# Landing figures of the load planner in a two-layer diffusion trunk: own values for stores, weights, reloaded operands and broadcast rows

## The chip, the cores and the metric

The kernel runs on one core of one Trainium2 chip. The metric is the device time of one execution in microseconds (us). Five engines work side by side on a core, each with its own queue of instructions: TensorE (PE: matmuls and transposes; its weight loads are listed as PEld), VectorE (DVE), ScalarE (ACT), GpSimd (POOL) and SyncE (SP). Here SP issues nearly all transfers (DMA). Data lie in HBM, in SBUF (128 partitions) and, for results of matmuls, in the eight banks of PSUM.

## The reference

One step of a diffusion model with two layers, for 128 context tokens and 512 latent tokens, model width 2048, all in float32. Per layer:

```python
shift, scale, gate = modulation(c, ada_w[l], ada_b[l])   # silu(c) @ w + b
h = rms_norm(x, norm_g[l]) * (1.0 + scale) + shift
y = mixer(h)                     # h @ w_in, branches, times silu(gate path)
x = x + gate * (y @ w_out[l])
```

Layer 0 mixes by windowed attention beside gated linear attention (GLA), layer 1 by neighbourhood attention beside a spatial-gating MLP (gMLP). A final norm follows. Context tokens have a conditioning vector of their own (`c_ctx`), so every modulation vector exists twice. Keys, values and the GLA states of the context are outputs too.

## The kernel before, in words

Activations are kept transposed: 16 tiles (k) of 128 features by 640 tokens. Every float32 operand of the large products is split into a high part in a rounded format and the remainder: `acth` and `actl` for activations, `whi` and `wlo` for weights. A product is then three matmuls (high by high, high by low, low by high) over two halves of 320 tokens. Later stages replace part of the plain products by Strassen-like ones, with sums of tiles in `eh`, `el`, `fh`, `fl`.

A weight tile of 128x512 goes through four steps: a load into `wraw`, `rs` or `adas` (SP), `whi` by ACT, `wlo` by POOL or DVE, matmuls by PE. Its slot in `wraw` can be loaded again when `wlo` is done.

Beside the matmuls runs a background task, `ada_task` (L1434), which works out the modulation vectors by dot products on DVE (and, while POOL helps, products on POOL that ACT sums up). It loads tiles of `ada_w` and, at the start of each column piece, two rows: the two conditioning vectors, each broadcast to all 128 partitions (`crow_s`; `shift_s` for the job "b0"). ACT copies each row to a PSUM bank. Three or four slots rotate, so the load that refills a slot is issued after the instruction that read it. The task runs the jobs "b0", "g0" (gate of layer 0) and "1" (shift and scale of layer 1) during layer 0, with pieces of 512 columns in `adas`; the job "g1" (gate of layer 1), with pieces of 256 columns in `rawx` and `small`, starts during layer 1 (`last_gate`, L2709). In the start, `shifts()` (L1622) does the same with `crow_b` and tiles `ada_s0`, while PE multiplies the tiles of `ada0` directly (L1599).

Between projections, `handover` (L1107) rewrites the operand of the next product: tiles which had been stored to HBM (`x1T_dram`, `yT_dram`) are loaded again, scaled where needed, split into `acth` and `actl`, and folded for the Strassen steps. PE needs them tile by tile. High and low parts of half an operand are also set aside in HBM and fetched back (`bh_dram`, `bl_dram`).

**What sets the order.** The order of instructions on every engine is made while the program is built, by a planner that keeps an estimated time of each engine (`Pace`, L56). Every operation that is emitted moves the estimated time of its engine on, and the estimated moment at which its output is ready is noted for each stretch of memory. `now` is the estimated time of PE. Generators for the side tasks are advanced in `tick` (L537) between matmuls. They ask the planner whether an operand is ready: `until` (L508) holds a task back until a tile is due within 0.05 us, and `wpump` (L748) emits a weight split only if its data are due within a lag. Nothing of this waits at run time: there, each engine takes its instructions in the order emitted, and semaphores hold an instruction until its operands are there.

Loads and stores go through `dma` (L473). A transfer whose operands are not ready by the estimate is put off; otherwise it is emitted, and its landing is estimated from the time `q` of the SP queue, the time `d` at which the DMA engines are free, the bytes, and a constant. The helpers `mm` and `tr` (L449 and L454 in the profile) emit matmuls and transposes; ACT, DVE and POOL instructions carry the line L219, and transfers L486.

Of the kernel before, what the change touches and what calls it, by code (L numbers as in the profile page):

```python
# [26 lines left out]
SPILL, YSP, KEEP, SHIFTS = "x1T_dram", "yT_dram", ("bh_dram", "bl_dram"), "shift_s"  # L27
# [218 lines left out]
class Trunk:  # L246
# [226 lines left out]
    def dma(self, out, in_):  # L473

        pc = self.pace
        o, i = [pc.span(out)], [pc.span(in_)]
        if pc.late:
            pc.due(o + i)
        n = int(np.prod(out.shape)) * 4
        rows = in_.name == SHIFTS  # L480

        def emit():
            at = pc.t["q"] = max(pc.t["q"], self.now, pc.ready("q", o, i)) + 0.45
            pc.t["d"] = max(pc.t["d"], at + 0.65) + max(0.09, n / 400e3)
            pc.note("q", o, i, pc.t["d"] + (self.ROWS if rows else 1.0))
            self.nc.sync.dma_start(out, in_)  # L486

        if pc.ready("q", o, i) <= self.now + 0.1:
            emit()
        else:  # L490
            pc.late.append((emit, o + i, lambda: pc.ready("q", o, i)))
# [2631 lines left out]
```

## Time and profile before

| What | Value |
|---|---|
| Median of 3 runs | 2054.4 us (2052.85 to 2056.66) |
| The profiled execution's own time | 2053.88 us |
| Its span, first to last instruction | 2052.1 us |
| Mean granted clock of TensorE | 0.997 |
| Instructions | 40329 |
| Moved by DMA | 344.13 MB, mean 168 GB/s |

The span is some 1.8 us shorter than the execution's time. The profile gives the busy time of each engine, the waits (who ended the idle time of whom), the chain of waits that ended last, the landing times of transfers, and any stretch of the timeline. "acth<-Y" means: writes acth, reads Y. A number in square brackets behind a row of the timeline is the idle time of that engine just before it, with what ended it. Stretches give for each engine the busy time and, in brackets, the count of instructions.

### The profile page before, as it was taken

The page shows a single profiled execution, that of the slowest core. Times are in us where ns is not written, and L with a number is a line of the kernel's source. Part 1 is how long each engine was busy: PE and PEld are TensorE (multiplying, and loading weights), DVE is VectorE, ACT ScalarE, POOL GpSimd, SP SyncE. Part 2 cuts the span into 40 slices and gives each one's busy share as a digit, 9 for nine tenths or more (in the row PEclk, how much of TensorE's full clock was granted, in tenths as well). Part 3 has the DMA queues.
Part 4 walks back from the last instruction along what each step waited for, and adds up shares of the span by engine and source line. Part 5 has one row for each costly group of instructions (what it writes and reads, how often), then busy time and mean ns, then how long its engine had stood idle before and what let it go on. Part 6 is the DMA issues. An engine that isn't in the chain of part 4 may idle for free.

```text
span 2052.1 us, 40329 instructions
## 1 busy us (share of the span) xinstructions
PE 2012.5 (98%) x14255; PEld 1975.3 (96%) x14255; DVE 1364.1 (66%) x3191; ACT 1093.2 (53%) x2414; POOL 1356.6 (66%) x1088
## 2 busy tenths in 40 slices
PE   8999999999999999999999999999999999999997
PEld 6899999999999999999989999999999999999997
DVE  4656578566667766897376787666666676568445
ACT  5445456444664765544465444555555654455443
POOL 4555345446456555888755777767766689878884
PEclk9999999999999999999999999999999999999999
DMA  9955333436567555575524434444344354266437
GB/s 381 394 206 167 120 105 107 129 114 203 154 210 225 171 169 179 192 230 188 188 92 149 127 117 134 143 132 134 110 154 132 116 165 151 92 216 195 146 95 277
DMA packets 234315, 344.13 MB, mean 168 GB/s; under 512 B 22048, under 2 KB 139648, under 8 KB 234112
## 3 DMA queue, kind: packets, MB, share of 16 engines
q1 hardware_dynamic: 232912, 340.38, 50.9%
q8 instruction: 112, 1.84, 0.4%
q10 hardware_dynamic: 1200, 1.17, 0.2%
q14 instruction: 91, 0.75, 0.1%
HBM read 304.99 MB, written 33.85 MB: 165 GB/s over the span
## 4 chain that ended last, share of the span: by engine, by line
PE 82%; DMA 9%; DVE 4%; ACT 2%; issue 1%; POOL 1%; SPq 0%; DVEq 0%; POOLq 0%; ACTq 0%
PE bank L449 80%; PE bank L454 2%; DMA more<-ada 1%; DMA Y<-xT 1%; DMA Y<-ada 1%; DMA wraw<-w_out 1%; DVE bank L219 1%; POOL wlo L219 1%; DMA wraw<-w_even 1%; DMA adas<-ada 1%; DMA raw<-ada_s 1%; DMA adas<-ada_g 1%; DVE adas L219 1%; DVE arena L219 1%; ACT whi L219 1%
## 5 line engine op out<-in xcount | busy, mean ns | idle before, releaser
L449 PE MATMUL bank<-acth,whi 128*128 128x320 f32 (+3 forms) x3072 | 939.8, 318 | 5.5 <-DVE YB L219 1.9
L449 PE MATMUL bank<-actl,whi 128*128 128x320 f32 (+3 forms) x3072 | 916.1, 310 | 2.0 <-POOL actl L219 2.0
L449 PE MATMUL bank<-acth,wlo 128*128 128x320 f32 (+3 forms) x3072 | 914.6, 310 | 0.3 <-POOL wlo L219 0.3
L219 POOL TENSOR_TENSOR wlo<-wraw,whi 128x512 fp32r<-128x512 f32 (+2 forms) x415 | 535.5, 1301 | 401.9 <-ACT whi L219 347.4
L449 PEld LDWEIGHTS bank<-acth,whi 128*128 128x128 f32 (+1 forms) x3072 | 568.5, 188 | 13.4 <-issue 4.1
L449 PEld LDWEIGHTS bank<-actl,whi 128*128 128x128 f32 (+1 forms) x3072 | 568.7, 188 | 4.7 <-POOL actl L219 2.8
L449 PEld LDWEIGHTS bank<-acth,wlo 128*128 128x128 f32 (+1 forms) x3072 | 567.8, 188 | 1.1 <-POOL wlo L219 1.1
L219 POOL TENSOR_TENSOR wlo<-rs,whi 128x384 fp32r<-128x384 f32 (+2 forms) x370 | 456.2, 1258 | 114.3 <-ACT whi L219 83.0
L219 ACT ACTIVATE whi<-wraw 128x512 fp32r<-128x512 f32 (+2 forms) x425 | 245.4, 586 | 146.6 <-PE bank L449 71.3
L219 ACT ACTIVATE whi<-rs 128x384 fp32r<-128x384 f32 (+2 forms) x370 | 189.7, 535 | 92.4 <-PE bank L449 46.7
L449 PE MATMUL bank<-eh,whi 128*128 128x322 f32 (+1 forms) x666 | 209.4, 314 | 0.0
L449 PE MATMUL bank<-eh,wlo 128*128 128x322 f32 (+1 forms) x666 | 206.6, 310 | 0.3 <-POOL wlo L219 0.3
L449 PE MATMUL bank<-el,whi 128*128 128x322 f32 (+1 forms) x666 | 206.4, 310 | 0.0
L219 POOL TENSOR_TENSOR prod<-adas,mixrow 128x512 f32<-128x512 f32 x87 | 113.2, 1311 | 48.6 <-ACT prod L219 34.3
L219 DVE TENSOR_TENSOR bank<-bank,sums 128x320 f32<-128x320 f32 (+1 forms) x148 | 70.1, 494 | 96.7 <-PE bank L449 46.3
L449 PEld LDWEIGHTS bank<-eh,wlo 128*128 128x128 f32 x666 | 125.3, 188 | 0.8 <-POOL wlo L219 0.6
L449 PEld LDWEIGHTS bank<-eh,whi 128*128 128x128 f32 x666 | 125.4, 188 | 0.0
L449 PEld LDWEIGHTS bank<-el,whi 128*128 128x128 f32 x666 | 125.3, 188 | 0.0
L219 DVE CUSTOM_DVE_ANT_0 adas<-adas,bank,part 128x512 bf16<-128x512 f32 x146 | 108.7, 744 | 23.4 <-DMA adas<-ada 20.5
L219 POOL TENSOR_TENSOR wlo<-adas,whi 128x512 fp32r<-128x512 f32 x62 | 81.3, 1317 | 35.4 <-ACT whi L219 26.9
L219 ACT ACTIVATE sums<-bank 128x320 f32<-128x320 f32 (+1 forms) x111 | 48.3, 435 | 99.7 <-PE bank L449 97.8
L219 DVE CUSTOM_DVE_ANT_0 old<-rawx,bank,partg 128x256 bf16<-128x256 f32 x140 | 66.8, 477 | 27.4 <-DMA rawx<-ada_g 24.2
(287 smaller groups left out, 3067.1 us busy)
## 6 DMA issues: line engine op xcount, KB each, us to landing
wraw<-w_even SPq DMA_DIRECT2D x176, 256.0 KB, 3.4
rs<-w_odd SPq DMA_DIRECT2D x150, 256.0 KB, 3.3
adas<-ada SPq DMA_DIRECT2D x128, 256.0 KB, 3.8
adas<-ada_g SPq DMA_DIRECT2D x64, 256.0 KB, 3.7
rs<-w_out SPq DMA_DIRECT2D x60, 256.0 KB, 3.5
adas<-w_odd SPq DMA_DIRECT2D x50, 256.0 KB, 3.7
Y<-ada SPq DMA_DIRECT2D x24, 512.0 KB, 7.8
more<-ada SPq DMA_DIRECT2D x24, 512.0 KB, 8.1
```

Of the source, the lines that this page charges most:

```text
L219: return f(*args, **kw)
L449: self.nc.tensor.matmul(out, lhsT, rhs, start=start, stop=stop, **kw)
L454: self.nc.tensor.transpose(out, in_, self.ident[:k, :k])
```

## The change

Only the estimate of a transfer's landing changes, in `dma`. Before, a transfer was taken as landed 1.0 us after the DMA engines had moved it, or 4.0 us (`ROWS`) for broadcast rows of `shift_s`. Now the constant depends on what is moved:

- a store to HBM: 1.0, as before;
- a row of `crow_s`, `crow_b` or `shift_s`: 3.5, and the DMA engines are taken as busy for 0.7 us more;
- a reload of a spilled operand (`x1T_dram`, `yT_dram`, `bh_dram`, `bl_dram`) or of the input `xT`: 1.6;
- every other load (weights, modulation tiles, constants, states, transfers within SBUF): 1.3.

```diff
         n = int(np.prod(out.shape)) * 4
-        rows = in_.name == SHIFTS
+        name, slow = in_.name, 0.0
+        if out.space == bass.MemoryType.DRAM:
+            land = 1.0
+        elif name in ("crow_s", "crow_b", SHIFTS):
+            land, slow = 3.5, 0.7
+        else:
+            land = 1.6 if name in (SPILL, YSP, *KEEP, "xT") else 1.3
 
         def emit():
             at = pc.t["q"] = max(pc.t["q"], self.now, pc.ready("q", o, i)) + 0.45
-            pc.t["d"] = max(pc.t["d"], at + 0.65) + max(0.09, n / 400e3)
-            pc.note("q", o, i, pc.t["d"] + (self.ROWS if rows else 1.0))
+            pc.t["d"] = max(pc.t["d"], at + 0.65) + max(0.09, n / 400e3) + slow
+            pc.note("q", o, i, pc.t["d"] + land)
             self.nc.sync.dma_start(out, in_)
```

`note` records when the outputs may be read and when the inputs may be overwritten; a reader on another engine is planned 0.22 us (`CROSS`) after that. `SPILL`, `YSP` and `KEEP` are the names of the HBM tensors listed above.

## The prediction

> **What bounds the kernel now.** I read the busy times first, then the stretches, then what TensorE (PE) waited for, then the chain of waits behind each stall. Busy times and the chain by engine, from the page:
>
> ```profile
> PE 2012.5 (98%) x14255; PEld 1975.3 (96%) x14255; DVE 1364.1 (66%) x3191; ACT 1093.2 (53%) x2414; POOL 1356.6 (66%) x1088
> ...
> PE 82%; DMA 9%; DVE 4%; ACT 2%; issue 1%; POOL 1%; SPq 0%; DVEq 0%; POOLq 0%; ACTq 0%
> ```
>
> PE is busy for 2012.5 of 2052.1 us, and the change alters no matmul. What can be won or lost is PE's idle time, 39.6 us. Its place, from the stretches of one page slice each (PE busy stands first after the length; PEclk, DMA share and GB/s last):
>
> ```profile
> 0.00:51.30 51.30, 42.14 (x497) 35.74 (x498) 22.35 (x49) 27.75 (x60) 25.47 (x32) 1.00 0.99 381
> 51.30:102.60 51.30, 47.46 (x557) 41.94 (x555) 30.91 (x80) 25.10 (x57) 30.24 (x22) 1.00 1.03 394
> ...
> 1026.00:1077.30 51.30, 46.89 (x303) 44.59 (x302) 37.71 (x67) 35.31 (x71) 27.93 (x19) 1.00 0.28 93
> ...
> 2000.70:2052.00 51.30, 38.28 (x249) 36.42 (x248) 25.67 (x47) 18.80 (x33) 23.54 (x25) 0.91 0.79 277
> ```
>
> The first two stretches lose 13.0 us while the DMA engines are full (0.99 and 1.03); the last loses 13.0, nearly all after the last matmul; the change of layer from 1026 on loses 4.4. The 9.2 that are left lie in single stalls. What PE waited for over the whole run (total, times, longest):
>
> ```profile
> PE bank L1599 <- DMA Y<-ada: 8.3, 4, 5.2
> PE bank L454 <- ACT arena L219: 3.7, 5, 1.7
> PE bank L454 <- ACT adas L219: 2.7, 1, 2.7
> PE bank L449 <- ACT acth L219: 2.0, 2, 1.1
> PE bank L449 <- POOL actl L219: 2.0, 2, 1.3
> PE bank L449 <- DVE YB L219: 1.9, 2, 1.2
> PE bank L449 <- ACT adas L219: 1.5, 3, 0.8
> PE bank L449 <- DVE bc L219: 1.2, 1, 1.2
> ```
>
> No stall after the start is for a DMA directly. But ACT, DVE and the SP queue run in order, so an instruction put too early, in front of a load that has not landed, holds everything behind it. That is what the planner's landing figures decide.
>
> **The change part by part.** The planner counts from the moment at which the SP queue is free: 0.45 us to issue, 0.65, bytes at 400 KB per us, then the landing figure. A 256 KB load is thus expected after 0.45+0.65+0.66+1.0 = 2.76 us; new: 3.06 for weights (1.3), and for a broadcast row of crow_s or crow_b 0.45+0.65+0.66+0.7+3.5 = 5.96 (128 KB: from 2.43 to 5.63). A 320 KB reload goes from 2.92 to 3.52. The rows of shift_s go from 5.76 to 5.96, and stores stay. The extra 0.7 also holds back every load planned behind a row. Measured, from issue to landing (median):
>
> ```profile
> wraw<-w_even SPq DMA_DIRECT2D x176, 256.0 KB, 3.4
> ...
> adas<-ada SPq DMA_DIRECT2D x128, 256.0 KB, 3.8
> ...
> adas<-crow_s SPq DMA_DIRECT2D x16, 256.0 KB, 4.3
> ...
> rawx<-crow_s SPq DMA_DIRECT2D x16, 128.0 KB, 3.7
> ...
> arena<-yT_dram SPq DMA_DIRECT2D x8, 320.0 KB, 5.3
> ```
>
> So weights were expected 0.6 us early, the reload 2.4, and both stay early; rows were 1.3 to 1.5 early and become 1.7 to 1.9 late. *No instruction, byte or matmul is added or removed*; the edit only reorders ACT, DVE, POOL and SP.
>
> *Rows, the clear case.* ACT and PE around 1127 us, where the modulation task for the second layer's gate begins with two rows:
>
> ```profile
> 1125.33 0.39 ACT L219 ACTIVATE bank<-rawx 128x256 f32<-128x256 f32 x1 [2.26 <-DMA rawx<-crow_s]
> 1126.66 0.39 ACT L219 ACTIVATE bank<-rawx 128x256 f32<-128x256 f32 x1 [0.94 <-DMA rawx<-crow_s]
> 1126.98 0.61 ACT L219 ACTIVATE whi<-rs 128x512 fp32r<-128x512 f32 x1
> 1127.50 0.71 ACT L219 ACTIVATE adas<-adas,bc 128x512 f32<-128x512 f32 x1
> 1128.26 0.98 PE L454 MATMUL bank<-ident,adas 128*128 128x128 f32 x4 [2.75 <-ACT adas L219]
> ```
>
> Two copies of rows, waiting 2.26+0.94 = 3.2 us, stand ahead of the copy of adas that PE's transposes need. The rows are now planned 3.2 us later, as much as ACT lost, so I take it that the adas copy goes first: 2.75 us saved. The load that refills a row's slot is issued behind the row's copy, so the SP queue moves with it, and weight loads pass it. The clock was lost with it:
>
> ```profile
> 1125.00:1130.00 5.00, 2.25 (x12) 1.98 (x11) 0.83 (x4) 3.22 (x7) 2.83 (x3) 0.84 0.76 252
> 1130.00:1135.00 5.00, 5.00 (x30) 5.00 (x29) 2.37 (x9) 1.34 (x3) 3.39 (x3) 0.81 0.17 52
> ```
>
> A granted 0.84 and 0.81 over 5 us each is 5x(0.16+0.19) = 1.75 us of PE's clock gone. Together 2.75+1.75 = 4.5.
>
> The Trainium skill ("TensorE: Matmul & The Clock Gate", Part 1) says that the clock halves after an idle window of about 3.4 us. Here 2.75 us of idle time sufficed, so the measurement decides; by that rule alone the term would be 2.75 and the forecast 1.75 us higher.
>
> *Rows, the other rounds.* Five more stalls of transposes (3.7 us in all, row above) lie before 740 us. For two of them the chain that released PE goes back to a load right behind two rows, and the tile view of crow_s tells who waited for rows:
>
> ```profile
> 643.87 4.75 DMA adas<-ada
> ...
> 667.36 0.33 PE bank L454
> 717.33 5.89 DMA adas<-ada
> ...
> 734.11 0.33 PE bank L454
> ```
>
> ```profile
>   ACT bank L219: 15.8, 9
> ```
>
> Those two loads took 4.75 and 5.89 us where 3.8 is the median, and DVE's first instruction on each tile waited. The planner had counted 2.76; now 3.06 and 1.4 for two rows ahead: 4.46. Between DVE's release and PE's stand some 11 to 19 us of other work, so not all comes back. Bounds: 0 and 3.7; I take 2.5, near the upper row, since the wait removed heads both chains.
>
> *Reloads.* At the first handover ACT and DVE wait together:
>
> ```profile
> 821.38 1.50 ACT L219 ACTIVATE acth<-arena 128x640 fp32r<-128x640 f32 x2 [3.98 <-DMA arena<-yT_dram]
> 821.45 0.50 DVE L219 TENSOR_TENSOR bank<-arena 128x320 f32<-128x320 f32 x1 [5.22 <-DMA arena<-yT_dram]
> ```
>
> Behind them stands DVE's copy for the gate (bc), PE's 1.2 us stall. The reload is planned 0.6 later, so a gain of 0 to 1.2; I take 0.6, one for one.
>
> *Weights, state, small loads* (+0.3): mostly loaded well ahead, and the split may be issued up to the lag (0.2 to 8 us) before the planned landing anyway; the cover is whi and wlo made earlier. Taken at 0; without that cover it is bounded by the start, next.
>
> *Start* (xT +0.6, crow_b +3.2, eight rows of 0.7 more): the DMA engines are full, so PE's 8.3 us for the ada tiles stay. PE's other idle time there is ended by DVE and ACT: 1.9 (YB), 1.5 (adas, line 449) and, of acth's 2.0, the 1.1 that the handover below does not hold: 4.5 us. The reordering can win these or add as much; taken at 0.
>
> *Handovers, the cost.* Waits of PE between 1020 and 1130 us beside adas (2.7) and actl (2.0, twice), then, from the costliest groups, the two engines' work on one weight split:
>
> ```profile
> PE bank L449 <- DVE Y L219: 0.9, 1, 0.9
> PE bank L449 <- ACT acth L219: 0.9, 1, 0.9
> PE bank L449 <- ACT bc L219: 0.5, 1, 0.5
> ```
>
> ```profile
> L219 POOL TENSOR_TENSOR wlo<-wraw,whi 128x512 fp32r<-128x512 f32 (+2 forms) x415 | 535.5, 1301 | 401.9 <-ACT whi L219 347.4
> ...
> L219 ACT ACTIVATE whi<-wraw 128x512 fp32r<-128x512 f32 (+2 forms) x425 | 245.4, 586 | 146.6 <-PE bank L449 71.3
> ```
>
> Here PE needs reloaded tiles rewritten as acth and actl. Planned 0.6 later, a rewrite can slip behind one weight split (0.59 on ACT, 1.30 on POOL). Bounds: 0, and 6x1.89 = 11.3 if it happens at these five stalls and the one at 826. I take two slips on ACT alone, 1.2: the shift is one split long.
>
> **Sum:** -4.5 -2.5 -0.6 +1.2 = -6.4. The profiled execution took 2053.88 us (span 2052.1), so 2047.5; the median of the runs shown, 2054.4, is 0.5 above it. Forecast **2048**.
>
> **The rivals.**
>
> *Stalls move and nothing is won.* Taking a wait off ACT helps only if what follows isn't held elsewhere. For it: DVE and POOL are 66% busy and PE's stalls are short. Against it: at 1126 only the two rows stand ahead. New stalls equal to the gain give about 2053.9.
>
> The Trainium skill ("DMA: Bandwidth & Descriptors", the two cost components) prices a transfer as about 2.0 us and its bytes at 436 GB/s, for which a row would be no different from a weight tile, about 2.6 us by estimate. By that rule the row figure corrects nothing and this rival holds; the traced 4.3 against 3.4 speaks against it.
>
> *Slower: handover rewrites fall behind weight splits.* The 11.3 us above against the same gains: 2047.5-1.2+11.3 = 2057.6, 2058 beside the median. It decides from four slips of six (7.56 us, as much as the gains' 4.5+2.5+0.6). For it: the stretch from 1026 already has four kinds of PE stall with ACT at 35.3 of 51.3 us. Against it: the weights are planned 0.3 later too, so the order between the two changes by half a split only.
>
> *The row figure is too long and the modulation work slides.* Last steps of that task:
>
> ```profile
> L219 DVE TENSOR_TENSOR part<-part,rawx x4: 511/874/1211, 954.1 to 956.5; 128x32 f32<-128x32 f32 x4
> L219 DVE CUSTOM_DVE_ANT_0 old<-rawx,bank,partg x140: 461/480/484, 1211.3 to 1698.6; 128x256 bf16<-128x256 f32 x140
> ```
>
> Eight rounds of rows after 284 us (both jobs that use crow_s), each at most 3.9 later (3.2 and 0.7), slide it by 31 us, to 988, before the layer change at 1026. Harmless, so it stays within the other cases.
>
> *The start gains too.* The 4.5 us there: 2047.5-4.5 = 2043.0.
>
> **Chances and range.** Forecast 0.38 (own range 2045 to 2051), nothing won 0.25, slower 0.24, start too 0.13. About 0.2% (4.1 us) is what a measurement of this kernel can tell from no change: faster means under 2050.3, slower over 2058.5. The forecast and the start give 0.49 faster and 0.02 same; nothing won gives 0.01, 0.22 and 0.02; the slower case, centred near the bound, 0.05 same and 0.19 slower (slips can also add clock loss as at 1128). So 0.50, 0.29, 0.21. For 8 in 10 the range reaches just past the start case and past the slower one: 2042 to 2060.
>
> **What would show it.** Right: ACT's waits for crow_s (15.8 us) nearly gone; the transposes at the g1 task's first rows without a stall, and no fall of the clock there; the chain at 667 and 734 without a load of ada. Wrong: the rows' waits gone but PE's idle time between 450 and 1130 us still near 13 us; new waits of PE for acth, actl or wlo at the handovers; a later end of the start, seen as PE idle over 14 us before 154 us. The forecast fails most surely if another stall of nearly 3 us appears and halves the clock again.

## The result, and the profile after

| | before | after |
|---|---|---|
| Median | 2056.66 us (2052.85 to 2062.10, 13 runs) | **2045.85 us** (2043.63 to 2052.22, 13 runs) |
| Ratio | 1 | **0.9949 [0.9936, 0.9962]** |
| Profiled execution | 2053.88 us | 2051.18 us (span 2049.4) |

The changed kernel is faster, by 2056.66 x 0.0051 = 10.5 us (7.8 to 13.2 by the interval). The first pair of traces shows only 2.7 us of that: the profiled execution of before was one of its quicker ones, that of after one of its slower ones. So I took one more trace of after (`a1_after`, 2046.89 us) and two more of before (`b1_before`, 2057.01; `b2_before`, 2056.14), and below I trust only what the traces of a kernel share.

After, the busy times and the chain by engine, from the page:

```profile
PE 2012.4 (98%) x14255; PEld 1976.9 (96%) x14255; DVE 1356.0 (66%) x3175; ACT 1098.7 (54%) x2430; POOL 1362.9 (67%) x1096
...
PE 87%; DMA 6%; DVE 3%; ACT 2%; issue 1%; POOL 1%; SPq 0%; DVEq 0%; POOLq 0%; ACTq 0%
```

PE's work is the same 2012.4 us (2012.5 before), as it must be. The chain that ended last now goes through PE for 87% instead of 82%, and through DMA for 6% instead of 9%: fewer waits that go back to a landing. The shares of PE are 82% in all three traces of before and 88% in `a1_after`. The same stretches as in the prediction (PE busy stands first after the length; clock, DMA share and GB/s last):

```profile
0.00:51.30 51.30, 41.74 (x498) 35.70 (x499) 22.42 (x45) 30.48 (x64) 26.33 (x33) 1.00 0.98 376
51.30:102.60 51.30, 46.91 (x556) 41.76 (x555) 35.32 (x84) 23.44 (x53) 30.18 (x22) 1.00 1.03 400
...
307.80:359.10 51.30, 49.27 (x331) 48.44 (x330) 36.72 (x58) 29.69 (x59) 25.50 (x18) 0.97 0.31 100
...
1026.00:1077.30 51.30, 47.52 (x302) 45.77 (x301) 36.98 (x65) 34.44 (x69) 27.01 (x19) 0.97 0.29 97
```

The first two stretches lose 14.0 us, no less than before (13.0). There is a stretch with idle time and a clock of 0.97 at 308 to 359, which is new, and one at the change of layer, with 3.8 us idle (4.4 before). What PE waited for over the whole run (total, times, longest):

```profile
PE bank L449 <- DVE bc L219: 2.8, 2, 2.0
...
PE bank L449 <- POOL actl L219: 1.3, 1, 1.3
PE bank L454 <- ACT adas L219: 1.2, 2, 0.8
...
PE bank L449 <- ACT acth L219: 0.9, 1, 0.9
PE bank L454 <- ACT arena L219: 0.7, 1, 0.7
```

Against before: the transposes (L454) waited 3.7 us for arena and 2.7 for adas, now 0.7 and 1.2. The wait for bc grew from 1.2 to 2.8, with one of 2.0 us. The waits for acth (2.0) and actl (2.0) read 0.9 and 1.3, but for actl the other two traces of before have 1.3 as well, so that fall is no effect of the change. PE's idle time by stretch, in all five traces (the first row from the stretches, the others the sum of the idle times in the timeline):

| us | before, three traces | after, two traces |
|---|---|---|
| 0 to 154 | 14.1, 14.9, 15.6 | 14.0, 12.8 |
| 154 to 800 | 3.7, 4.2, 3.2 | 4.0, 2.0 |
| 800 to 1000 | 1.2, 1.4, 1.3 | 1.2, 2.0 |
| 1000 to 1100 | 4.4, 3.7, 3.4 | 3.8, 3.3 |
| 1100 to 1300 | 3.1, 3.4, 3.4 | 1.2, 0.0 |

Only the last row separates the kernels clearly in every trace. There, at the first rows of job "g1", ACT's timeline of after reads (start, duration, instruction, idle before it):

```profile
1124.74 0.72 ACT L219 ACTIVATE adas<-adas,bc 128x512 f32<-128x512 f32 x1 [0.25 <-DVE adas L219]
...
1126.80 0.77 ACT L219 ACTIVATE Y<-bank 128x512 f32<-128x512 f32 x2 [0.79 <-PE bank L454]
1127.45 0.82 ACT L219 ACTIVATE bank<-rawx 128x256 f32<-128x256 f32 x2
```

The copy of adas goes at 1124.74, ahead of both row copies, which go together at 1127.45 without a wait; before, it went at 1127.50, behind them. And the clock there (stretches of 5 us, columns as above):

```profile
1125.00:1130.00 5.00, 5.00 (x37) 4.99 (x37) 0.00 (x0) 3.54 (x8) 5.00 (x5) 1.00 0.83 255
1130.00:1135.00 5.00, 5.00 (x36) 5.00 (x35) 4.25 (x10) 1.17 (x4) 2.20 (x3) 1.00 0.05 18
```

PE is busy for all of both stretches at a granted 1.00, where it had 2.25 us of work in the first and 0.84 and 0.81 in clock.

### The profile page after: what moved, and what is told of

Its sections match the earlier page's. It is cut to its first block, busy times and chain, and to the rows that moved or that the text cites. A ratio compares the mean times of both kernels' runs of the same rounds, so it can differ in the third digit from the quotient of the medians.

```text
span 2049.4 us, 40331 instructions
## 1 busy us (share of the span) xinstructions
PE 2012.4 (98%) x14255; PEld 1976.9 (96%) x14255; DVE 1356.0 (66%) x3175; ACT 1098.7 (54%) x2430; POOL 1362.9 (67%) x1096
## 4 chain that ended last, share of the span: by engine, by line
PE 87%; DMA 6%; DVE 3%; ACT 2%; issue 1%; POOL 1%; SPq 0%; DVEq 0%; POOLq 0%; ACTq 0%
PE bank L449 84%; PE bank L454 2%; DMA more<-ada 1%; DMA Y<-ada 1%; DVE bank L219 1%; DVE arena L219 1%; DVE Y L219 1%; DMA arena<-yT_dram 1%; PE bank L1605 0%; DMA Y<-xT 0%; ACT acth L219 0%; DMA wraw<-w_even 0%; DMA wraw<-w_out 0%; DVE rs L219 0%; DMA rawx<-ada_g 0%
## 5 line engine op out<-in xcount | busy, mean ns | idle before, releaser
L219 POOL TENSOR_TENSOR prod<-adas,mixrow 128x512 f32<-128x512 f32 x93 | 121.1, 1313 | 50.6 <-ACT prod L219 32.4
L219 DVE CUSTOM_DVE_ANT_0 adas<-adas,bank,part 128x512 bf16<-128x512 f32 x146 | 108.6, 744 | 22.6 <-DMA adas<-ada 15.7
L219 DVE CUSTOM_DVE_ANT_0 adas<-adas,bank 128x512 bf16<-128x512 f32 x107 | 73.2, 684 | 13.6 <-DMA adas<-ada 5.2
```

What stands on the lines that cost most here:

```text
L219: return f(*args, **kw)
```

## The experiments

Two theories stood against each other. By the first, that of the prediction, an estimate that covers the real landing keeps ACT and DVE from being blocked by an instruction whose load is late, and the rows carry the gain. By the second, the old order was merely an unlucky draw: any change of the estimates shuffles thousands of instructions, and most shuffles would have helped. The first expects the parts to gain where their own waits go, and wrong estimates to cost; the second expects gains from any nudge. "Change" below means against before in the same comparison, in us by its median and interval.

| Kernel | Median us | Ratio to before | Change us |
|---|---|---|---|
| `e1_rows` | 2047.29 | 0.9937 [0.9913, 0.9960] | -13.0 (-17.9 to -8.2) |
| `e2_loads` | 2055.01 | 0.9975 [0.9959, 0.9991] | -5.1 (-8.4 to -1.9) |
| `e3_crow_b` | 2054.98 | 0.9971 [0.9955, 0.9987] | -6.0 (-9.3 to -2.7) |
| `e4_crow_s` | 2052.82 | 0.9963 [0.9948, 0.9978] | -7.6 (-10.7 to -4.5) |
| `e5_g1_rows` | 2053.98 | 0.9983 [0.9970, 0.9996] | -3.5 (-6.2 to -0.8) |
| `a1_after` | 2046.77 | 0.9947 [0.9930, 0.9964] | -10.9 (-14.4 to -7.4) |
| `e6_early` | 2064.52 | 1.0037 [1.0024, 1.0049] | +7.6 (+4.9 to +10.1) |
| `e7_issue` | 2058.62 | 1.0018 [1.0009, 1.0028] | +3.7 (+1.9 to +5.8) |
| `e8_rows_median` | 2045.80 | 0.9949 [0.9933, 0.9964] | -10.5 (-13.8 to -7.4) |
| `e9_reload_long` | 2052.07 | 0.9978 [0.9967, 0.9990] | -4.5 (-6.8 to -2.1) |

### Rows alone, and the other loads alone

`e1_rows`: the three kinds of rows as in the change, everything else at 1.0.

```diff
+        name, slow, land = in_.name, 0.0, 1.0
...
+        elif name in ("crow_s", "crow_b", SHIFTS):
+            land, slow = 3.5, 0.7
...
+            pc.t["d"] = max(pc.t["d"], at + 0.65) + max(0.09, n / 400e3) + slow
+            pc.note("q", o, i, pc.t["d"] + land)
```

> Only the broadcast rows get their new figures (3.5 and 0.7 for crow_s, crow_b and shift_s); weights, reloads and all else stay at 1.0. Theory A, the rows carry the gain: ratio to before 0.994 to 0.997, ACT's waits for crow_s (15.8 us before) under 4 us, and no stall of nearly 3 us of PE for adas near 1128 us. Theory B, the figures of weights and reloads carry it: ratio 0.998 to 1.001. Theory C, any reordering would do, the order before was an unlucky draw: the ratio is like that of the other partial changes of this call.

`e2_loads`: the rows at their old figures, weights and the like at 1.3, reloads and xT at 1.6.

```diff
+        name, slow, land = in_.name, 0.0, 1.3
+        if out.space == bass.MemoryType.DRAM:
+            land = 1.0
+        elif name in ("crow_s", "crow_b"):
+            land = 1.0
+        elif name == SHIFTS:
+            land = 4.0
+        elif name in (SPILL, YSP, *KEEP, "xT"):
+            land = 1.6
```

> Only weights, modulation tiles and small loads (1.3) and reloads and xT (1.6) get their new figures; the rows stay as before (1.0 for crow_s and crow_b, 4.0 for shift_s). Theory A: ratio 0.998 to 1.001, ACT still waits 10 us or more for crow_s, and PE's stall of 2.75 us near 1128 us is still there. Theory B: 0.994 to 0.997, with less idle time of ACT before reloaded tiles. Theory C: like the others.

The rows alone give 0.9937, as much as the whole change (0.9947 to 0.9949). The other loads alone give 0.9975, which lies between the ranges of its theories A and B, yet on top of the rows they add nothing that can be seen. PE's wait for adas at 1100 to 1170 us and ACT's waits for crow_s in `e2_loads`:

```profile
PE bank L454 <- ACT adas L219: 3.1, 1, 3.1
```

```profile
  ACT bank L219: 22.6, 14
```

and the same two in `e1_rows`:

```profile
PE bank L454 <- ACT adas L219: 1.2, 2, 0.9
```

```profile
  ACT bank L219: 1.2, 1
```

With the old row figure the stall of about 3 us at the g1 rows stays and ACT waits 22.6 us for rows (15.8 before); with the new one both go. So those waits belong to the row figure.

### Which rows

`e3_crow_b` and `e4_crow_s` give the new figures to one of the two kinds only, `e5_g1_rows` only to the rows of 256 columns of job "g1"; `shift_s` keeps its 4.0. Against `e1_rows`, the three edits one below the other:

```diff
-        elif name in ("crow_s", "crow_b", SHIFTS):
+        elif name in ("crow_b",):
...
+        elif name in ("crow_s",):
...
+        elif name == "crow_s" and out.shape[-1] == 256:
             land, slow = 3.5, 0.7
```

> Only the rows of the start (crow_b) get 3.5 and 0.7; all else is as before. Theory A by the prediction's terms: the start was put at nothing, so 0.999 to 1.001. Rival: the start carries it; PE's idle time before 154 us (14.1 us before) falls by 3 us or more and the ratio is 0.996 to 0.998.

> Only the rows of the modulation task (crow_s) get 3.5 and 0.7; all else is as before, so the order up to about 280 us is that of before. Theory A: most of the gain, 0.995 to 0.998 (4.5 us at the first rows of the second layer's gate, 2.5 at the rounds before), with ACT's waits for crow_s nearly gone. Rival, stalls only move: 0.999 to 1.001 with ACT's waits for crow_s gone all the same.

> Only the rows of the job g1 (the 256-column pieces of crow_s, from about 1119 us on) get 3.5 and 0.7; the order up to there is that of before. The prediction's term for this place is 4.5 us (2.75 of stall, 1.75 of clock): time at 1150 us earlier by 3.5 to 4.5 than in before's trace, and a ratio of about 0.998. Rival, the gain is given back by a later wait: earlier by 3.5 or more at 1150 us and by 1 or less at 1300 us, ratio 0.9995 to 1.0005.

**crow_s** gives -7.6 us, the g1 job -3.5 of it. PE's wait for adas at 1100 to 1170 us, first in `e4_crow_s`, then in `e5_g1_rows`, then in `e3_crow_b`:

```profile
PE bank L454 <- ACT adas L219: 1.2, 1, 1.2
```

```profile
PE bank L454 <- ACT adas L219: 1.6, 2, 0.9
```

```profile
PE bank L454 <- ACT adas L219: 2.7, 1, 2.7
```

The stall goes in both kernels that treat these rows and stays in the one that does not. Over all traces the split is clean: PE's wait for adas there is one stall of 2.7 to 3.1 us in the seven whose rows of "g1" have the old figure (before three times, `e2_loads`, `e3_crow_b`, `e6_early`, `e7_issue`), and in the seven that have the new one at most 1.6 us in all, in stalls of 1.2 us or less, although the order ahead of it differs among the kernels on both sides. ACT's waits for crow_s over the whole run, in `e4_crow_s`, `e5_g1_rows` and `e3_crow_b`:

```profile
  ACT bank L219: 2.7, 1
```

```profile
  ACT bank L219: 10.0, 7
```

```profile
  ACT bank L219: 11.3, 8
```

In `e5_g1_rows`, where the pieces of 512 columns keep the old figure, 10.0 us of waits are left; in `e4_crow_s` 2.7. The largest of PE's waits from 154 to 1000 us in `e4_crow_s`:

```profile
PE bank L454 <- ACT arena L219: 1.8, 2, 1.2
```

Two stalls of transposes are left (1.8 us) of the five with 3.7. That is not shown to be the work of the row figure: this wait is also down to 2.2 us in `e2_loads`, 1.6 in `e3_crow_b` and 1.3 in `e7_issue`, which leave crow_s alone. It is smallest, 0 to 0.7 us, where all rows have new figures.

**crow_b** is used in the start only, and gives -6.0 us. How it gains is not shown. ACT was hardly blocked by these rows themselves; its wait for crow_b in before, from the tile view:

```profile
  ACT bank L219: 0.4, 1
```

What changes is ACT's wait for the tiles of xT, here in before, in `e3_crow_b`, in `e4_crow_s`, and in `e7_issue` (a nudge of 0.02 us per issue, described below):

```profile
  ACT acth L219: 21.5, 13
```

```profile
  ACT acth L219: 10.0, 10
```

```profile
  ACT acth L219: 23.1, 13
```

```profile
  ACT acth L219: 8.5, 6
```

They halve with the new figure for crow_b (10.5 in after) and not with that for crow_s. But they also fall where the start is merely reordered by estimates that are no truer: to 15.1 in `e6_early` and to 8.5 in `e7_issue`, two kernels that did not gain. So in the start the old order was an unlucky one for this wait, and the wait alone does not carry the gain. The first matmul of the GLA norm is a mark that all kernels share; here are its rows in before and `e3_crow_b` (first and last start behind the durations in ns), and PE's work up to it in both:

```profile
L449 PE MATMUL bank<-gx,rawx x16: 430/432/433, 247.5 to 464.5; 128*128 128x320 f32 x16
```

```profile
L449 PE MATMUL bank<-gx,rawx x16: 430/432/433, 242.4 to 463.5; 128*128 128x320 f32 x16
```

```profile
0.00:247.50 247.50, 233.44 (x2133) 218.50 (x2134) 135.47 (x310) 124.49 (x269) 128.25 (x112) 1.00 0.72 259
```

```profile
0.00:242.40 242.40, 229.86 (x2121) 216.55 (x2122) 137.23 (x310) 127.82 (x277) 135.05 (x117) 1.00 0.75 268
```

The three traces of before reach it at 247.5 to 249.3; `e3_crow_b` at 242.4 and after at 244.3 (`a1_after` 243.8, `e1_rows` 242.9), while `e4_crow_s` (249.1) and `e5_g1_rows` (250.1) are like before. Against the mean of the three, 248.6, the matmul comes 4 to 6 us earlier with crow_b.

Not all of that is time won. Twelve matmuls of the projection (2133 against 2121, in after as in `e3_crow_b`) stand behind the mark instead of ahead of it; at 0.147 us from one to the next they are 1.8 us. Counted to the same number of matmuls, 2133, `e3_crow_b`, `e1_rows`, `a1_after` and after lead the mean of before by 3.9, 3.4, 2.5 and 2.0 us. Nor does it take the figure for crow_b: `e2_loads` (243.9) and `e6_early` (245.7) reach the mark early too, and `e7_issue` (249.0) does not.

The last of these matmuls comes at 463.5 in `e3_crow_b` and at 466.3 in after, against 464.5 to 466.3 in before: part of the gain has been given back by then. Where, PE's waits from 154 to 1000 us in `e3_crow_b` tell, and DVE's timeline of after behind them:

```profile
PE bank L449 <- ACT eh L219: 2.4, 1, 2.4
PE bank L449 <- DVE bc L219: 2.0, 1, 2.0
```

```profile
342.08 2.46 DVE L219 TENSOR_TENSOR_SCAN Y<-arena,Y 128x640 f32<-128x640 f32 x1
...
344.85 0.14 DVE L219 TENSOR_SCALAR bc<-bank 128x2 f32<-128x2 f32 x1
```

The copy of the gate (bc, 0.14 us) is queued on DVE behind a scan of 2.46 us; PE waits 2.03 us for it in after, and 2.0 in `e3_crow_b`, `a1_after` and `e1_rows`. Before has no such stall there (its one wait for bc is the 1.2 us at 826). It is the new wait that takes part of the start's gain. The clock pays again, in after:

```profile
345.00:350.00 5.00, 4.96 (x24) 4.92 (x25) 4.16 (x7) 3.47 (x9) 0.00 (x0) 0.66 0.04 16
```

0.66 over 5 us is 1.7 us of clock lost. The wait for eh in `e3_crow_b` (2.4 us) lies at 828 us, at the first handover, and is in no trace of after; `e4_crow_s` and `e7_issue` have one there too (1.6 and 2.7). The whole new loss is 2.03 + 1.7 = 3.7 us, in after and `a1_after`; in `e1_rows`, `e3_crow_b` and `e9_reload_long` the same stall left the clock alone.

The traces thus do not show where the 6.0 us come from. The traced execution of `e3_crow_b` took 2056.28 us, as much as those of before (2053.88 to 2057.01), so its gain stands in the medians only. And PE's idle time before 154 us fell from 14.1 to 12.5 us, not by the 3 us that the expectation had asked of a gain in the start.

By their medians the parts add: -7.6 for crow_s and -6.0 for crow_b make -13.6, and all rows together give -13.0.

### The same kernels again

`b1_before`, `b2_before` and `a1_after` are before and after without an edit.

> The kernel before, unchanged, for a second trace of it: its runs span 15 us (2052 to 2067), and the trace so far is of one of 2053.9. If the spread arises in the start (DMA-bound), the two traces differ by the end of the start and run parallel after it; if it is PE's clock, the stretches of low clock differ; if it is stalls anywhere, they differ step by step.

> The same once more, for the same question: a third trace of the kernel before.

> The changed kernel, unchanged, on the same chip and in the same rounds as the others of this call: ratio 0.993 to 0.997. With it a second trace: if the long wait for the gate's copy at 343 us and the low clock behind it belong to the order, they come again; if they are chance, not.

The ratio of after was repeated (0.9947). The stall at the g1 rows is there in both new traces of before (3.07 and 3.01 us) and absent in `a1_after`. Its low clock is not always there: at 1130 to 1135 us, first `b1_before`, then `b2_before`,

```profile
1130.00:1135.00 5.00, 4.09 (x29) 4.09 (x30) 3.01 (x9) 3.41 (x7) 3.93 (x4) 1.00 0.35 116
```

```profile
1130.00:1135.00 5.00, 5.00 (x27) 5.00 (x28) 3.19 (x11) 2.24 (x5) 3.63 (x3) 0.71 0.25 81
```

the first kept a granted 1.00 and the second fell to 0.71. So the clock's part of that stall is paid in two of three executions here, about 1.2 us on the mean of them rather than 1.75. With the four other kernels that have the stall it is four of seven.

### Is it chance?

`e6_early`: before, with all landings of loads taken 0.3 us earlier. `e7_issue`: before, with 0.47 us instead of 0.45 for each issue, which moves estimates by a negligible amount and reorders all the same.

```diff
-            pc.note("q", o, i, pc.t["d"] + (self.ROWS if rows else 1.0))
+            pc.note("q", o, i, pc.t["d"] + (3.7 if rows else 1.0 if out.space == bass.MemoryType.DRAM else 0.7))
```

```diff
-            at = pc.t["q"] = max(pc.t["q"], self.now, pc.ready("q", o, i)) + 0.45
+            at = pc.t["q"] = max(pc.t["q"], self.now, pc.ready("q", o, i)) + 0.47
```

> The kernel before with every load taken as landed 0.3 us earlier (0.7, rows of shift_s 3.7; stores stay at 1.0): further from what is measured. Theory A, the gain comes from planning where loads really land: ratio 1.000 to 1.004. Theory C, the order before was an unlucky draw and any reordering gains: 0.996 to 0.999, as for the loads' own figures (0.9975).

> The kernel before with 0.47 in place of 0.45 us for an issue on the SP queue: a nudge of 0.02 us that makes no landing more or less true. Theory A: within 0.998 to 1.002 of before, on either side. Theory C: 0.996 to 0.999. PE's stall of nearly 3 us near 1128 us comes again by A.

Estimates that are still earlier cost 7.6 us, and the small nudge cost 3.7. Neither gained, so for the kernel as a whole these two do not bear the second theory out, and at the g1 rows it falls, as the stall stays in every order with the old figure. For the start it is not refuted: there both kernels cut ACT's waits for xT (15.1 and 8.5 against 21.5 us), and `e6_early` came to the GLA norm early. The nudge also shows that a shuffle without a reason is worth about 0.2%, and a gain of that size, such as that of `e2_loads`, cannot be put down to one cause; of the 6.0 us of `e3_crow_b`, whose interval reaches down to 2.7, that holds as well. In `e7_issue` the g1 stall (2.7 us) and ACT's waits for rows (20.1) stay.

### How long the figures must be

`e8_rows_median`: after, with 2.0 instead of 3.5 for rows. `e9_reload_long`: after, with 2.6 instead of 1.6 for reloads and xT.

```diff
-            land, slow = 3.5, 0.7
+            land, slow = 2.0, 0.7
```

```diff
-            land = 1.6 if name in (SPILL, YSP, *KEEP, "xT") else 1.3
+            land = 2.6 if name in (SPILL, YSP, *KEEP, "xT") else 1.3
```

> The changed kernel with 2.0 in place of 3.5 for broadcast rows: a row is planned at 4.46 us after its issue is due, about the measured median of crow_s (4.3). If the row figure has only to reach the median: 0.993 to 0.996, like the changed kernel. If it must cover late rows: ACT's waits for crow_s rise from 1.6 us to 5 or more, and the ratio goes to 0.996 to 0.998.

> The changed kernel with 2.6 in place of 1.6 for reloads and xT, nearer to the measured 5.3 us of arena<-yT_dram. If true landings are what counts everywhere: ACT's and DVE's waits for reloads (8.6 and 3.9 us in the changed kernel's first trace) fall by half or more and the ratio is 0.991 to 0.994, better than the changed kernel. If the slower rival's mechanism holds (rewrites fall behind weight splits), PE's stalls at the handovers grow by 1.9 us each and the ratio is 0.996 to 0.999.

With 2.0 a row of 256 KB is planned at 0.45+0.65+0.66+0.7+2.0 = 4.46 us, just over the traced median of 4.3, and the time is the same as with 3.5: 0.9949 both. ACT's waits for crow_s and PE's for adas at 1100 to 1170 us in `e8_rows_median`:

```profile
  ACT bank L219: 5.4, 5
```

```profile
PE bank L454 <- ACT adas L219: 0.7, 1, 0.7
```

ACT waits 5.4 us again and PE not: for crow_s, to cover the median is enough. The 0.7 us that a row holds the planned DMA engines longer was in every kernel with a row figure and was not tried apart.

For reloads the same logic did not hold. 2.6 brings the planned 3.52 us for a 320 KB reload to 4.5, nearer to the 5.3 that the trace of before has as its median, and yet half the gain is lost (0.9978). The loss is in the start. PE's waits from 0 to 154 us in `e9_reload_long`:

```profile
PE bank L1605 <- DMA Y<-ada: 8.9, 4, 5.9
PE bank L449 <- DVE actl L219: 4.6, 2, 2.8
```

Two stalls for actl, 4.6 us, are new (0.2 in after, over the whole run), and the clock was low behind each. The start uses the figure only through xT. At the handover, where reloads count, nothing was seen to be worse: 4.4 us of PE idle time from 1000 to 1100, as in the trace of before. Nor was it better: the waits for yT_dram of ACT and DVE went from 6.9 and 3.9 us in after to 5.9 and 3.0, not down by half. Since one figure served both, reloads and xT were not told apart.

## Why the prediction was right, and where a term was mis-sized

The forecast was 2048, and 2045.85 was measured: right in direction and range, and in the mechanism for the rows of job "g1". Of the gain it had 6.4 us, and 7.8 to 13.2 were measured, so a term was missing. That the times lie only 2.2 us apart is in part luck: the forecast started from a median of 2054.4 over three runs of before, which is 2056.66 over thirteen.

- **Rows of job "g1", -4.5 predicted.** The mechanism is as described: the adas copy passes the row copies, and the stall and its low clock go. By the 8000th matmul, near 1130 us, all seven kernels with the new figure for these rows have gained 3.2 to 3.3 us since the 7500th on the mean of the three traces of before, and the four others with the old one 0.3 at most. `e5_g1_rows` measured -3.5 (-6.2 to -0.8). The clock's 1.75 us were too high a price, as the low clock followed in four of seven executions only.
- **Other rounds of rows, -2.5.** What crow_s gives beyond "g1" is 7.6-3.5 = 4.1 us, though with the two intervals this is only rough. With the first term it is -7.6 against the predicted -7.0. The mechanism of this term is not shown. It had the wait of ACT right (15.8 to 2.7 us in `e4_crow_s`), but PE's stalls of transposes, by which it was priced, fell to 1.8 us there and to 1.3 to 2.2 in three kernels with the old figure. In `e4_crow_s` the chain ahead of the stall at 668 us still holds two loads of ada. So the nearness of the size is luck as far as is known.
- **Reloads, -0.6.** The stall of PE at 826 us, 1.16, 1.43 and 1.33 in the three traces of before, is 0.76 and 0.86 in the two of after: -0.5. In the other traces with the new reload figure (`e2_loads`, `e8_rows_median`, `e9_reload_long`) PE has no stall there, in the other six with the old one 0.5 to 2.7 us, so the term is borne out, though the order of the rest moves this stall as much. ACT's first reload in after shows why, in its timeline:

```profile
820.50 0.74 ACT L219 ACTIVATE acth<-arena 128x640 fp32r<-128x640 f32 x1 [2.21 <-DMA arena<-yT_dram]
```

  It waits 2.21 us where it had waited 3.98. It is still planned early.
- **Start, taken at 0: the mis-sized term.** crow_b alone is worth -6.0 us (-9.3 to -2.7), beyond the bound of 4.5 by its median. I had set the bound by PE's visible stalls that DVE or ACT ended. The row of waits for xT, 21.5 us of ACT, would not have priced it either, since in `e7_issue` it falls to 8.5 and nothing is won. Only a part of the gain is PE idle time. From 100 to 154 us before and `e3_crow_b` have

```profile
100.00:154.00 54.00, 52.94 (x478) 50.16 (x477) 27.31 (x75) 22.08 (x51) 26.29 (x23) 1.00 0.62 216
```

```profile
100.00:154.00 54.00, 54.00 (x489) 51.67 (x488) 28.14 (x79) 23.89 (x57) 28.17 (x25) 1.00 0.68 225
```

  that is 1.1 us of idle time less and eleven matmuls more. Summed over 0 to 154 us in the same way, the idle time is 14.1, 14.9 and 15.6 us in the traces of before, and 14.0, 12.8, 13.3 and 12.5 in after, `a1_after`, `e1_rows` and `e3_crow_b`: 1.7 less on the mean. With the 1.8 us of matmuls that moved behind it, this is 3.5 of the 5.2 us by which the GLA norm begins earlier on the mean of the four. The rest does not stand as idle time, and where it lies is not shown; nor is it shown that the figure works by covering the landings of crow_b, and not by a better draw of the start's order.
- **Weights and small loads, taken at 0.** On top of the rows nothing is seen (0.9947 and 0.9949 against 0.9937 for rows alone, with intervals that overlap). Alone they, with reloads and xT, gave -5.1; by the nudge's 3.7 us no more than a part of that can have a cause of its own.
- **Handovers, +1.2.** Not seen: PE's idle time from 1000 to 1100 us is 3.8 and 3.3 in after against 3.4 to 4.4. The slower rival, four rewrites behind weight splits, did not come. PE's waits of 0.94 us for acth and 1.29 for actl at this handover stand in all 14 traces.
- **The rivals.** "Stalls move and nothing is won" holds at one place: the 2.03 us behind the scan at 345 us, with 1.7 us of clock, 3.7 us that `e1_rows` and `e3_crow_b` paid only in part. The rule of the Trainium skill ("DMA: Bandwidth & Descriptors", the two cost components) that this rival was given is fitted there to transfers issued by GpSimd. Here SP issues them, and the traced 4.3 us for a row against 3.4 for a weight tile of as many bytes decides. "The start gains too" is what happened by the medians, though not by the stalls that it was priced by; 2045.85 lies between the forecast and its 2043.0. The modulation work slid and did no harm, as worked out: in layer 0 its last step comes at 979.8 instead of 956.5 us (988 was the bound). Its last step of all in after, from the tile view of rawx:

```profile
L219 DVE CUSTOM_DVE_ANT_0 old<-rawx,bank,partg x140: 461/481/485, 1220.6 to 1717.5; 128x256 bf16<-128x256 f32 x140
```

  comes for the last time at 1717.5 instead of 1698.6, some 300 us before the end.
- **What would show it.** ACT's waits for crow_s did go nearly to nothing, in after:

```profile
  ACT bank L219: 1.6, 2
```

  The chain no longer goes through a load of ada at 667 and 734 us; from after:

```profile
626.50 41.66 PE bank L449 x282
...
733.60 4.63 PE bank L449 x32
```

  PE's idle time from 450 to 1130 us fell from 12.0 us in before to 6.9 in after and 5.5 in `a1_after`, and the start did not end later (14.0 and 12.8 us idle before 154). The sign against the forecast, "another stall of nearly 3 us that halves the clock again", did come in a smaller form, at 345 us, and cost a part of the gain only.

Still open: how the figure for crow_b gains, and whether another order of the start would gain as much; whether the figures for weights and reloads are worth anything beside the rows; and why `e1_rows` (2047.29) and `e8_rows_median` (2045.80), which differ from after by a few figures, cannot be told from it. None of them is shown to beat it.

## What to carry to other kernels

Where the order is fixed ahead and engines run in order, look in the trace for an instruction that waits for a late load with something behind it that the bottleneck needs, and plan that kind of load just above its median landing: here two row copies ahead of one copy cost PE about 3 us in every order with the old figure, and a longer figure than the median brought no more. That is shown for one kind of row; for reloads and xT a figure nearer to the median lost half of the gain. A shorter wait of an engine behind the bottleneck is no proof of a gain: ACT's wait for xT fell by more than half in a kernel that became slower. And compare times at a mark only where the same work stands ahead of it. In a kernel whose order a planner makes, measure a nudge that means nothing as well: here it moved the time by 0.18%, and an edit that is worth no more than that tells nothing on its cause.

## What the runs showed of the hardware

**Short stalls can cost clock, and not each time.** The row of 345 to 350 us above has 0.66 behind a single idle time of 2.03 us. At the change of layer, two idle times close together did it. PE's timeline of before, where they are followed by no loss, and the stretch of 5 us behind them in before and in `b1_before`:

```profile
1057.05 0.56 PE L449 MATMUL bank<-acth,whi 128*128 128x322 f32 x2 [0.94 <-ACT acth L219]
...
1058.90 0.56 PE L449 MATMUL bank<-actl,whi 128*128 128x322 f32 x2 [1.29 <-POOL actl L219]
...
1061.66 0.56 PE L449 MATMUL bank<-actl,whi 128*128 128x322 f32 x2 [0.72 <-POOL actl L219]
```

```profile
1060.00:1065.00 5.00, 4.28 (x28) 3.85 (x27) 4.84 (x6) 2.59 (x6) 3.17 (x3) 1.00 0.31 105
```

```profile
1060.00:1065.00 5.00, 3.77 (x16) 3.77 (x17) 2.54 (x3) 4.89 (x10) 3.94 (x3) 0.66 0.16 54
```

The same pair (0.94 and 1.29 us, in `b1_before` 2.3 us later than here) left the clock at 1.00 in one execution of the same kernel and took it to 0.66 in another; it stands in all 14 traces, and nine of them lost the clock behind it. Each loss is 5 x 0.34 = 1.7 us, a low stretch of 3.4 us at half speed (in stretches of 1 us the granted clock there is 0.50). So a stall of 2 us has a price of 2 or of 3.7 us from one execution to the next. Part of it can come back: the third stall, 0.72 us, is missing in the nine, since a slower PE comes later to the operand it would have waited for, which leaves a net 1.0.

The Trainium skill ("TensorE: Matmul & The Clock Gate", Part 1) says that the monitor watches a free-running activity window of about 3.4 us and that the clock halves after an idle window. The length of the low stretches here agrees; a wholly idle window was not needed, since 2.03 us, and 0.94 and 1.29 us with work between them, sufficed, and there the measurement decides.

**One kernel's executions differ by more than many edits.** Before ranged from 2050 to 2067 us on one core over all comparisons, 0.8%. Chance in the clock explains some 1.7 us for each place where it may fall; the rest was not traced.
